# The even layer's TensorE order, written out: attention in clusters between whole channel products

## The chip, the cores and the metric

The kernel runs on one core of a Trainium2 chip. The metric is the time of one execution in microseconds, the median of several; lower is better. The engines are named as in the profile: PE (TensorE matmuls), PEld (its weight loads), DVE (VectorE), ACT (ScalarE), POOL (GpSimd) and SP (SyncE, which here only issues DMAs).

## The reference

One inference step of two layers for 384 tokens: 256 of a prompt and 8 samples of 16. The change lies in the mixer of the first (even) layer:

```python
def even_mixer(h, ck, cv, clogf, sconv_state, w_in, conv_w, q_gain, k_gain, b_f, w_out):
    proj = h @ w_in
    gate_b, gate_c, u, q, k, v, f_logit = jnp.split(proj, cuts, axis=-1)
    conv_out, new_sconv = causal_dwconv(gate_c * u, sconv_state, conv_w)
    a_out = gate_b * conv_out
    q = rms_norm(q.reshape(hs), q_gain)
    k = rms_norm(k.reshape(hs), k_gain)
    ...
    attn = fox_attention(q, k_all, v_all, logf_all, n_past).reshape(b, length, FOX_WIDTH)
    out = jnp.concatenate([a_out, attn.astype(a_out.dtype)], axis=-1) @ w_out
```

So one half is a gated short convolution over 512 channels, the other an attention of 8 heads of 64 with a decay: the score of query and key gets the difference of their summed log-forget values, is masked causally, and goes through a softmax. The prompt attends to itself (256 x 256 a head), each sample to its 128 cached keys and its own 16. After the mixer come a feed-forward block (FFN), then the odd layer and its FFN; these are the same in both kernels.

## The kernel before

All activations lie feature-major: 128 channels on the partitions, 384 tokens along the free axis. A product in full precision is made of three matmuls: activations and weights are split into a high part that PE takes in its fast format (Hh, wh) and a rest (Hl, wl), and `three` adds wh·Hh, wh·Hl and wl·Hh. A weight tile of 128 x 1024 comes by a DMA on SP (raw), ACT rounds it (wh), DVE subtracts (wl). raw, wh and wl have three buffers each, and one tile holds the weights of one whole channel product.

The even layer, in the order of its source:

- q, k and v, token-major, by `tm_group`: eight weight pieces of 512 columns for three token tiles each. `qk` squares and sums the heads, scales, and leaves q and k in SBUF (the tiles qraw, kraw). `to_features` transposes them on PE (qT, kT), four 128x128 a token tile; ACT writes QT and KTt. POOL then scales kraw in place and stores it (o_k); ACT writes vt from v, POOL stores it (o_v).
- `short_conv(i)`, i from 0 to 3: three channel products of 24 matmuls each (gc, gu, gb), 128 x 384, and then the convolution on DVE, ACT and POOL (tiles cu, cpad, cc, cg, ca), which writes rows 0 to 3 of yh and yl, the two parts of the output projection's input.
- Prompt attention by blocks. The first has 128 queries, 128 keys, and all 8 heads; the second block of queries has 256 keys, and two groups of four heads. A block's scores (s) lie in two PSUM banks, one for the even heads and one for the odd (`par`): the decay (cumP with nid8R, or cum0 with onesR), the mask (causR with identR), and then KTt with QT, 64 rows of the array for each parity. DVE takes the maximum (mx), ACT the exponential with its sum (pr), DVE the reciprocal (rs) and the scaling (pr); PE transposes pr (pt), DVE copies it out (pts), and PE multiplies by vt (po), 64 columns of the array for each parity.
- The samples: scores in groups of three, three and two (ss), softmax (prs), transposes (pt, pn), the products with cached and new values (pa), and transposes of the result (aoT), which end in rows 4 to 7 of yh and yl.
- The output projection op, eight tiles of 24 matmuls, in halves: rows 0 to 3 and rows 4 to 7.

Each attention step has several calls of `fill`, which would draw channel products from the generator `beside_attention`. Its ratio FILL_E is 0.0, so all of them are written behind attention, by `fill.rest()`. A scheduler that works on the written program decides the order on each engine: PE's order before is its choice. `T.keep` ties PE's instructions to the source order where it is set; it is not set in the kernel before. Weight tiles are made at high priority.

The pools: `e1` holds what is needed up to v (kraw, krow, lfA among them), `e2` takes its memory afterwards and holds what convolution and attention need (onesR, cum0, cpad, pr and others), so e2's first tiles wait for the last use of e1's, o_k's DMAs among them. Eight PSUM banks: four for large products (`pmm`: v, gc, gu, gb, op) and four for the rest (`paux`: kT, s, pt, po, ss, pa).

Of the kernel before, what the change touches and what calls it, by code (L numbers as in the profile page):

```python
# [10 lines left out]
F32 = mybir.dt.float32  # L11
# [219 lines left out]
def build(nc, tc, d, stop=None):  # L231
# [38 lines left out]
    def paux(name):  # L270
        return psum["aux"].tile([P, 512], F32, tag="aux", name=name)
# [11 lines left out]
    def prc(name, i):  # L283
        o = COL[name] + i
        return prm[:, o:o + 1]
# [10 lines left out]
    def f32(ap):  # L296
        return ap.bitcast(F32)

    def tt(out, a, b, op, eng=None):
        (eng or V).tensor_tensor(out=out, in0=a, in1=b, op=op)  # L300
# [4 lines left out]
    def act(out, a, f, **kw):  # L305
        S.activation(out, a, f, **kw)  # L306
# [294 lines left out]
    def to_features(src, name, fill=None):  # L601

        ps = paux(name)
        for i in range(4):
            T.transpose(ps[:, i * P:(i + 1) * P], src[:, i * P:(i + 1) * P], ident)
        if fill:
            fill(4)
        return ps.rearrange("p (k t) -> p k t", t=P)
# [39 lines left out]
                    rows = slice(64 * half, 64 * half + 64)  # L648
                    V.tensor_scalar_mul(Qb[rows, kt, :, 16 * half:16 * half + 16], tok_s(ps[rows, kt, :]), qg8[rows, :])
    k = qk("k")  # L650
    for b in range(3):
        ps = to_features(k[:, b, :], "kT")
        act(KTt[:, :, b * P:(b + 1) * P], ps, AF.Copy, scale=prc("kg", 0))
        tt(k[:, b, :], k[:, b, :], krow, ALU.mult, G)
        nc.gpsimd.dma_start(out=d["o_k"][b], in_=k[:, b, :])

    ps = run(tm_group("v"))
    for b in range(3):
        act(vt[:, b, :], ps[b], AF.Copy, scale=r[:, b:b + 1])
        nc.gpsimd.dma_start(out=d["o_v"][b], in_=vt[:, b, :])  # L660
    e1s.close()

    e2s = ExitStack()
    e2 = e2s.enter_context(tc.tile_pool(name="e2", bufs=2))

    def short_conv(i):
        pg, pu, pb = pmm("gc"), pmm("gu"), pmm("gb")
# [36 lines left out]

    fill = Fill(beside_attention(), FILL_E)

    def softmax(ps3, out3, sums):

        n = len(sums)
        nm = tiny.tile([P, n], F32, tag="mx", name="mx")  # L710
        V.reduce_max(out=nm, in_=ps3, axis=AX.X, negate=True)
        for i in range(n):
            act(out3[:, i, :], ps3[:, i, :], AF.Exp, bias=nm[:, i:i + 1], accum_out=sums[i])
# [6 lines left out]
        tt(cum0[:, par, :, :], f32(cumP[:, 0:P]).unsqueeze(1).broadcast_to([P, 4, P]),  # L720
           C("nid8")[:, par::2].unsqueeze(2).broadcast_to([P, 4, P]), ALU.mult)

    for qb in range(2):
        nk = P * (qb + 1)
        nh = 512 // nk
        po = paux("po").rearrange("p (k t) -> p k t", t=P)
        for h0 in range(0, 8, 2 * nh):
            banks = [paux("s").rearrange("p (h k) -> p h k", k=nk) for _ in range(2)]
            for par in range(2):
                if qb == 0:  # L730
                    T.matmul(banks[par], lhsT=onesR, rhs=cum0[:, par, :, :], start=True, stop=False)
                    fill()
                else:
                    for i in range(nh):
                        h = h0 + 2 * i + par
                        T.matmul(banks[par][:, i, :], lhsT=nid8R[:, h:h + 1].broadcast_to([P, P]), rhs=cumP[:, 0:nk],
                                 start=i == 0, stop=False)
                        fill()
                T.matmul(banks[par][:, :, nk - P:nk], lhsT=identR, rhs=causR.unsqueeze(1).broadcast_to([P, nh, P]),
                         start=False, stop=False)  # L740
                fill()
            for i in range(nh):
                for par in range(2):
                    kt = (h0 + 2 * i) // 2
                    rows = slice(64 * par, 64 * par + 64)
                    T.matmul(banks[par][:, i, :], lhsT=QT[rows, kt, qb * P:(qb + 1) * P], rhs=KTt[rows, kt, 0:nk],
                             start=False, stop=i == nh - 1)
                    fill()
            pts = []
            for par in range(2):  # L750
                pr = e2.tile([P, nh, nk], F32, tag="pr", name="pr")
                sm = tiny.tile([P, nh], F32, tag="sm", name="sm")
                softmax(banks[par], pr, [sm[:, i:i + 1] for i in range(nh)])
                rs = tiny.tile([P, nh], F32, tag="rs", name="rs")
                V.reciprocal(rs, sm)
                tt(pr, pr, rs.unsqueeze(2).broadcast_to([P, nh, nk]), ALU.mult)
                pt = paux("pt")
                for i in range(nh):
                    for kb in range(qb + 1):
                        o = (i * (qb + 1) + kb) * P  # L760
                        T.transpose(pt[:, o:o + P], pr[:, i, kb * P:(kb + 1) * P], ident)
                        fill()
                ptt = e2.tile([P, 512], F32, tag="pts", name="pts", bufs=3)
                V.tensor_copy(ptt, pt)
                pts.append(ptt)
            for i in range(nh):
                kt = h0 // 2 + i
                for kb in range(qb + 1):
                    o = (i * (qb + 1) + kb) * P
                    for par in range(2):  # L770
                        h = 2 * kt + par
                        T.matmul(po[64 * par:64 * par + 64, kt, :], lhsT=vt[:, kb, 64 * h:64 * h + 64],
                                 rhs=pts[par][:, o:o + P], start=kt == 0 and kb == 0, stop=kt == 3 and kb == qb)
                        fill()
        o = slice(qb * P, (qb + 1) * P)
        act(yh[:, 4:8, o], po, AF.Copy)
        tt(yl[:, 4:8, o], po, f32(yh[:, 4:8, o]), ALU.subtract)


    pn = e2.tile([P, NB, LB], F32, name="pn", bufs=1)  # L780
    pTp = e2.tile([P, NB, P], F32, name="pTp", bufs=1)
    rS = e2.tile([P, NB], F32, name="rS", bufs=1)
    for b0 in range(0, NB, 3):
        nb = min(3, NB - b0)
        ps = paux("ss")
        s3 = ps[:, :nb * 144].rearrange("p (b k) -> p b k", k=144)
        T.matmul(ps[:, :nb * 144], lhsT=nidSR, rhs=cumS[:, 144 * b0:144 * (b0 + nb)], start=True, stop=False)
        fill()
        T.matmul(s3[:, :, P:144], lhsT=identR, rhs=smaskR.unsqueeze(1).broadcast_to([P, nb, LB]), start=False, stop=False)
        fill()  # L790
        for i in range(nb):
            b = b0 + i
            kc = e0.tile([P, 4, P], F32, tag="kvc", name="kc", bufs=4)
            nc.sync.dma_start(out=kc, in_=d["kc"][b])
            for new in range(2):
                for kt in range(4):
                    rows = slice(32 * kt, 32 * kt + 32)
                    if new:
                        T.matmul(s3[rows, i, P:144], lhsT=Qb[:, kt, b, :], rhs=KTt[:, kt, 256 + LB * b:256 + LB * (b + 1)],
                                 start=False, stop=i == nb - 1)  # L800
                        fill()
                    else:
                        T.matmul(s3[rows, i, 0:P], lhsT=Qb[:, kt, b, :], rhs=kc[:, kt, :], start=False, stop=False)
                        fill()
        pr = e2.tile([P, nb, 144], F32, tag="prs", name="prs")
        sm = tiny.tile([P, nb], F32, tag="sms", name="sms")
        softmax(s3, pr, [sm[:, i:i + 1] for i in range(nb)])
        V.reciprocal(rS[:, b0:b0 + nb], sm)
        V.tensor_copy(pn[:, b0:b0 + nb, :], pr[:, :, P:144])
        pt = paux("pt")  # L810
        for i in range(nb):
            T.transpose(pt[:, i * P:(i + 1) * P], pr[:, i, 0:P], ident)
            fill()
        V.tensor_copy(pTp[:, b0:b0 + nb, :], pt[:, :nb * P].rearrange("p (b k) -> p b k", k=P))
    ps = paux("pn")
    T.transpose(ps[:, 0:P], pn.rearrange("p b t -> p (b t)"), ident)
    fill()
# [2 lines left out]
    pTm = e2.tile([P, NB, P], F32, name="pTm", bufs=1)  # L820
    for b in range(NB):
        V.tensor_scalar_mul(pTm[:, b, :], pnT, C("bmask")[:, b:b + 1])
    for j in range(2):
        pa = paux("pa")
        for i in range(4):
            b = 4 * j + i
# [2 lines left out]
            for new in range(2):  # L829
                for kt in range(4):  # L830
# [2 lines left out]
                    T.matmul(pa[32 * kt:32 * kt + 32, i * P:(i + 1) * P], lhsT=lhs, rhs=rhs,  # L833
                             start=i == 0 and not new, stop=i == 3 and new == 1)
                    fill()
        ao = e2.tile([P, 4, P], F32, tag="ao", name="ao", bufs=1)
        tt(ao, pa.rearrange("p (b c) -> p b c", c=P), rS[:, 4 * j:4 * j + 4].unsqueeze(2).broadcast_to([P, 4, P]), ALU.mult)
        ps = paux("aoT")
        for i in range(4):
            T.transpose(ps[:, i * P:(i + 1) * P], ao[:, i, :], ident)  # L840
            fill()
        for half in range(2):
# [4 lines left out]
            act(oh, src, AF.Copy)  # L847
            tt(yl[rows, 4:8, o].rearrange("p k (b t) -> p k b t", t=LB), src, f32(oh), ALU.subtract)

    fill.rest()  # L850
    for m0 in (0, 4):
        ps = ops if m0 == 0 else [pmm("op") for _ in range(4)]
        for m in range(4):
            if m0:
                run(fm_group(ps[m], yh, yl, range(0, 4), True, False))
        for m in range(4):
            run(fm_group(ps[m], yh, yl, range(4, 8), False, True))
            residual(m0 + m, ps[m])
            norm_tile(m0 + m, "g_ffn", 0, e2)
# [496 lines left out]
```

## Time and profile before

| | |
|---|---|
| median of 3 runs | 1062.48 us (1061.84 to 1063.17) |
| the profiled execution | 1065.19 us, of which 1063.4 is the span of its instructions |
| granted PE clock, mean | 0.995 |
| PE, PEld, DVE, ACT, POOL busy | 98%, 91%, 70%, 48%, 10% of the span |
| even layer from v's end to the FFN's first matmul | 65.24 to 183.62 us |

A row of the timeline gives the start in us from the span's start, the length in us, the engine, the line, the operation, out<-in by tile names without buffer numbers, the shapes, and the count; in brackets the idle time of that engine before it and what ended it. Matmuls are pipelined, so the lengths of neighbours overlap: what one costs PE is the distance from its start to the next start. A matmul in f32 shows as two records. All matmuls are made by `Tensor.matmul`, on line 240 (transposes on 245), so a matmul is told by its tiles. L300 is the two-tensor operation of DVE or POOL, L303 its form with a scalar, L306 any ACT operation. A row of the table by stretches has the stretch, its length, busy time (and count) of PE, PEld, DVE, ACT and POOL, PE's granted clock, the share of the DMA engines and GB/s.

### The profile page before, as it was taken

What the parts mean: (1) busy time and instruction counts of PE and PEld (TensorE: products, weight loads), DVE (VectorE), ACT (ScalarE), POOL (GpSimd) and SP (SyncE); (2) the same over time, 40 slices, a digit from 0 to 9 for tenths busy, and PEclk for the clock granted to TensorE, in tenths of its full rate; (3) what the DMA queues carried; (4) which work ended last, traced back from release to release, by engine and by line L of the source; (5) the groups of instructions that cost most, each with busy time, mean ns of one, the idle gap of its engine ahead of it and who ended that gap; (6) DMA issues with size and microseconds to landing.
All of it is one profiled execution on the core that took longest, in us unless ns stands there. A gap on an engine that the chain in (4) does not pass through costs nothing.

```text
span 1063.4 us, 16718 instructions
## 1 busy us (share of the span) xinstructions
PE 1039.9 (98%) x6316; PEld 969.7 (91%) x6316; DVE 739.8 (70%) x1361; ACT 511.6 (48%) x855; POOL 104.4 (10%) x339
## 2 busy tenths in 40 slices
PE   9999999999999999999899999899999999999998
PEld 6788799999999999989678888787989999999998
DVE  6967657777777734458989979868987776665331
ACT  5444335444444433346968668364544444443221
POOL 0030010100000000013313112210001100000000
PEclk9999999999999999999999999999999999999999
DMA  7542434344343443435555463553533434434541
GB/s 261 170 158 81 160 112 128 126 122 137 119 132 127 130 136 119 126 108 167 188 187 190 159 198 130 190 179 103 179 125 120 127 120 123 133 122 135 151 136 43
DMA packets 50329, 150.31 MB, mean 141 GB/s; under 512 B 5992, under 2 KB 8312, under 8 KB 50248
## 3 DMA queue, kind: packets, MB, share of 16 engines
q1 hardware_dynamic: 44360, 136.78, 40.9%
q10 hardware_dynamic: 4608, 8.39, 2.1%
q0 software_dynamic: 1280, 4.06, 1.0%
q8 instruction: 50, 0.82, 0.3%
q14 instruction: 31, 0.25, 0.1%
HBM read 135.81 MB, written 13.40 MB: 140 GB/s over the span
## 4 chain that ended last, share of the span: by engine, by line
PE 38%; DVE 13%; ACT 3%; issue 2%; DMA 0%; ACTq 0%; DVEq 0%
PE fg L240 9%; PE fd L240 9%; PE fa L240 8%; PE z L240 4%; PE xbc L240 3%; DVE wl L300 2%; DVE c L303 2%; PE op L240 2%; DVE wl L303 1%; DVE X L300 1%; ACT wh L306 1%; PE y L240 1%; DVE pad L300 1%; PE S L240 0%; ACT L306 0%
## 5 line engine op out<-in xcount | busy, mean ns | idle before, releaser
L300 DVE TENSOR_TENSOR wl<-raw,wh 128x1024 fp32r<-128x1024 f32 (+1 forms) x205 | 252.5, 1232 | 140.6 <-ACT wh L306 140.1
L306 ACT ACTIVATE wh<-raw 128x1024 fp32r<-128x1024 f32 (+1 forms) x205 | 216.0, 1054 | 225.0 <-PE fd L240 95.0
L240 PE MATMUL fg<-Hh,wh 128*128 128x384 f32 x352 | 119.0, 338 | 1.0 <-DVE pad L300 1.0
L240 PE MATMUL fa<-Hl,wh 128*128 128x384 f32 x352 | 119.3, 339 | 0.6 <-DVE Hl L303 0.6
L240 PE MATMUL fg<-Hl,wh 128*128 128x384 f32 x352 | 119.2, 339 | 0.0
L240 PE MATMUL fa<-Hh,wl 128*128 128x384 f32 x352 | 119.0, 338 | 0.0
L240 PE MATMUL fg<-Hh,wl 128*128 128x384 f32 x352 | 119.0, 338 | 0.0
L240 PE MATMUL fa<-Hh,wh 128*128 128x384 f32 x352 | 118.9, 338 | 0.0
L240 PE MATMUL fd<-hh,wh 128*128 128x384 f32 x352 | 118.3, 336 | 0.0
L240 PE MATMUL fd<-hh,wl 128*128 128x384 f32 x352 | 118.3, 336 | 0.0
L240 PE MATMUL fd<-hl,wh 128*128 128x384 f32 x352 | 118.3, 336 | 0.0
L303 DVE SCALAR_TENSOR_TENSOR c<-pad,prm,c 128x400 f32<-128x400 f32 (+1 forms) x160 | 101.9, 645 | 7.9 <-ACT c L306 6.2
L240 PEld LDWEIGHTS fg<-Hh,wh 128*128 128x128 f32 x352 | 66.2, 188 | 1.3 <-ACT R L306 1.3
L240 PEld LDWEIGHTS fa<-Hl,wh 128*128 128x128 f32 x352 | 66.1, 188 | 1.1 <-DVE Hl L303 0.9
L240 PE MATMUL xbc<-Hh,wh 128*128 128x384 f32 x192 | 65.9, 343 | 0.7 <-DVE X L300 0.7
L240 PEld LDWEIGHTS fa<-Hh,wl 128*128 128x128 f32 x352 | 66.2, 188 | 0.1
L240 PEld LDWEIGHTS fg<-Hl,wh 128*128 128x128 f32 x352 | 66.2, 188 | 0.1
L240 PEld LDWEIGHTS fg<-Hh,wl 128*128 128x128 f32 x352 | 66.2, 188 | 0.1
L240 PEld LDWEIGHTS fa<-Hh,wh 128*128 128x128 f32 x352 | 66.1, 188 | 0.1
L240 PEld LDWEIGHTS fd<-hh,wh 128*128 128x128 f32 x352 | 66.2, 188 | 0.0
L240 PEld LDWEIGHTS fd<-hl,wh 128*128 128x128 f32 x352 | 66.2, 188 | 0.0
L240 PEld LDWEIGHTS fd<-hh,wl 128*128 128x128 f32 x352 | 66.2, 188 | 0.0
(737 smaller groups left out, 2108.1 us busy)
## 6 DMA issues: line engine op xcount, KB each, us to landing
raw<-w SPq DMA_DIRECT2D x219, 512.0 KB, 3.5
kc<-kc SPq DMA_DIRECT2D x8, 256.0 KB, 3.5
vc<-vc SPq DMA_DIRECT2D x8, 256.0 KB, 3.0
X<-x SPq DMA_DIRECT2D x8, 192.0 KB, 4.7
o_y<-X SPq DMA_DIRECT2D x8, 192.0 KB, 2.8
o_v<-vt POOLq DMA_DIRECT2D x3, 256.0 KB, 2.5
o_k<-kraw POOLq DMA_DIRECT2D x3, 256.0 KB, 3.3
cst<-cst SPq DMA_DIRECT2D x1, 617.0 KB, 5.9
```

Source lines behind the costliest of these rows:

```text
L240: ins = nc.tensor.matmul(*a, **kw)
L300: (eng or V).tensor_tensor(out=out, in0=a, in1=b, op=op)
L303: V.scalar_tensor_tensor(out=out, in0=a, scalar=s, in1=b, op0=op0, op1=op1)
L306: S.activation(out, a, f, **kw)
```

## The change

From v on, PE's instructions are tied to the source order, and the source is written in the order wanted. `dense()` draws eight pieces from `beside_attention`, that is one whole channel product; the attention steps stand between, as `Heads(qb, h0)` (scores and softmax of one block), `turn` (transposes) and `out` (values), and as `scores`, `turn_scores`, `samples_out` and `turn_out` for the samples. v is written ahead of k's transposes, and kraw's pool closes behind them. pr gets four buffers instead of two, ao two instead of one.

```diff
     k = qk("k")
-    for b in range(3):
-        ps = to_features(k[:, b, :], "kT")
-        ...
     ps = run(tm_group("v"))
     for b in range(3):
         act(vt[:, b, :], ps[b], AF.Copy, scale=r[:, b:b + 1])
         nc.gpsimd.dma_start(out=d["o_v"][b], in_=vt[:, b, :])
-    e1s.close()
...
+    def dense(n=8):
+        for _ in range(n):
+            next(fill.gen, None)
+
+    T.keep = True
+    dense()
+    for b in range(3):
+        ps = to_features(k[:, b, :], "kT")
+        act(KTt[:, :, b * P:(b + 1) * P], ps, AF.Copy, scale=prc("kg", 0))
+        tt(k[:, b, :], k[:, b, :], krow, ALU.mult, G)
+        nc.gpsimd.dma_start(out=d["o_k"][b], in_=k[:, b, :])
+
+    e1s.close()
+
+    e2s = ExitStack()
+    e2 = e2s.enter_context(tc.tile_pool(name="e2", bufs=2))
+    dense(16)
...
+    class Heads:
+        def __init__(self, qb, h0):
...
+            for i in range(nh):
+                for par in range(2):
+                    T.matmul(banks[par][:, i, :], lhsT=QT[rows, kt, ...], rhs=KTt[rows, kt, 0:nk], ...)
...
+    first = Heads(0, 0)
+    dense()
+    second = Heads(1, 0)
+    first.turn()
+    dense()
+    po = pout()
+    first.out(po)
+    second.turn()
+    dense()
+    third = Heads(1, 4)
+    po = pout()
+    second.out(po)
+    dense()
+    third.turn()
...
+    s0 = scores(0)
+    dense()
+    third.out(po)
+    s1 = scores(3)
+    turn_scores(*s0)
+    dense()
+    s2 = scores(6)
+    turn_scores(*s1)
+    dense()
+    turn_scores(*s2)
...
+    dense()
+    a0 = samples_out(0)
+    dense()
+    a1 = samples_out(1)
+    turn_out(*a0)
+    dense()
+    turn_out(*a1)
     fill.rest()
+    T.keep = False
```

Three places show how the instructions move. The first is PE behind v's last matmul. Before, where v_640 is v's third token tile:

```order
L240 MATMUL v_640<-wl,Hh 128x512
L240 MATMUL v_640<-wh,Hl 128x512
L240 MATMUL gc<-Hh,wh 128x384
L245 MATMUL kT<-cst,kraw 128x128 x4
L240 MATMUL gc<-Hl,wh 128x384
L245 MATMUL kT<-cst,kraw 128x128 x4
L240 MATMUL gc<-Hh,wl 128x384
L245 MATMUL kT<-cst,kraw 128x128 x4
```

In the change, the end of the first gc product and the start of gu:

```order
L240 MATMUL gc<-Hh,wh 128x384
L240 MATMUL gc<-Hl,wh 128x384
L240 MATMUL gc<-Hh,wl 128x384
L245 MATMUL kT<-cst,kraw 128x128 x12
L240 MATMUL gu<-Hh,wh 128x384
```

The twelve transposes stand behind the whole gc product instead of behind its first matmul.

The second is DVE ahead of the first block's decay, between the scaling of kraw and cum0 (cum_749 before, cum_842 in the change). Before:

```order
L300 TENSOR_TENSOR kraw<-kraw,hs_609 128x512 x3
L300 TENSOR_TENSOR wl<-raw,wh 128x1024 x3
L717 CAST onesR<-cst 128x128
L300 TENSOR_TENSOR cum_749<-cumP,cst 128x512
L300 TENSOR_TENSOR wl<-raw,wh 128x1024
L300 TENSOR_TENSOR cum_749<-cumP,cst 128x512
```

In the change:

```order
L300 TENSOR_TENSOR kraw<-kraw,hs_609 128x512 x3
L300 TENSOR_TENSOR wl<-raw,wh 128x1024 x4
L726 CAST onesR<-cst 128x128
L300 TENSOR_TENSOR cum_842<-cumP,cst 128x512 x2
L300 TENSOR_TENSOR cu<-gu,R_232 128x384
```

One more weight tail stands ahead of onesR and cum0.

The third is PE at the second block. Before, from the second bank of the first block's transposes on:

```order
L245 MATMUL pt<-cst,pr 128x128 x4
L240 MATMUL gu<-Hh,wh 128x384
L240 MATMUL po<-pts,vt 64x128
L240 MATMUL s<-cumP,nid8R 128x256 x2
L240 MATMUL s<-causR,identR 128x2x128
L240 MATMUL s<-cumP,nid8R 128x256 x2
L240 MATMUL s<-causR,identR 128x2x128
L240 MATMUL s<-KTt,QT 128x256 x2
L240 MATMUL po<-pts,vt 64x128 x7
L240 MATMUL s<-KTt,QT 128x256 x2
L240 MATMUL gu<-Hl,wh 128x384
```

In the change, from the end of the second gc product on:

```order
L240 MATMUL gc<-Hh,wl 128x384
L240 MATMUL s<-cumP,nid8R 128x256 x2
L240 MATMUL s<-causR,identR 128x2x128
L240 MATMUL s<-cumP,nid8R 128x256 x2
L240 MATMUL s<-causR,identR 128x2x128
L240 MATMUL s<-KTt,QT 128x256 x4
L245 MATMUL pt<-cst,pr 128x128 x8
L240 MATMUL gu<-Hh,wh 128x384
```

The block's scores stand in one piece, with the first block's eight transposes behind them; its po follows after the whole gu product. The eight KTt matmuls of the first block, four of one parity and then four of the other before, alternate between the parities in the change.

More of the change, by code (lines that the diff above doesn't have):

```diff
@@ L650, in build @@
     k = qk("k")
-    for b in range(3):
-        ps = to_features(k[:, b, :], "kT")
-        act(KTt[:, :, b * P:(b + 1) * P], ps, AF.Copy, scale=prc("kg", 0))
-        tt(k[:, b, :], k[:, b, :], krow, ALU.mult, G)
-        nc.gpsimd.dma_start(out=d["o_k"][b], in_=k[:, b, :])
     ps = run(tm_group("v"))
@@ L660, in build @@
         nc.gpsimd.dma_start(out=d["o_v"][b], in_=vt[:, b, :])
-    e1s.close()
-    e2s = ExitStack()
-    e2 = e2s.enter_context(tc.tile_pool(name="e2", bufs=2))
     def short_conv(i):
@@ L721, in build @@
            C("nid8")[:, par::2].unsqueeze(2).broadcast_to([P, 4, P]), ALU.mult)
[L723 to L728, printed above, removed]
+    class Heads:
+        def __init__(self, qb, h0):
+            self.qb, self.h0, self.nk = qb, h0, P * (qb + 1)
+            self.nh = nh = 512 // self.nk
+            nk = self.nk
+            self.banks = banks = [paux("s").rearrange("p (h k) -> p h k", k=nk) for _ in range(2)]
             for par in range(2):
@@ L731, in build @@
                     T.matmul(banks[par], lhsT=onesR, rhs=cum0[:, par, :, :], start=True, stop=False)
-                    fill()
                 else:
@@ L747, in build @@
                              start=False, stop=i == nh - 1)
-                    fill()
-            pts = []
+            self.prs = []
             for par in range(2):
-                pr = e2.tile([P, nh, nk], F32, tag="pr", name="pr")
+                pr = e2.tile([P, nh, nk], F32, tag="pr", name="pr", bufs=4)
                 sm = tiny.tile([P, nh], F32, tag="sm", name="sm")
@@ L756, in build, with turn, out @@
                 tt(pr, pr, rs.unsqueeze(2).broadcast_to([P, nh, nk]), ALU.mult)
+                self.prs.append(pr)
+        def turn(self):
+            self.pts = []
+            for pr in self.prs:
                 pt = paux("pt")
-                for i in range(nh):
-                    for kb in range(qb + 1):
-                        o = (i * (qb + 1) + kb) * P
+                for i in range(self.nh):
+                    for kb in range(self.qb + 1):
+                        o = (i * (self.qb + 1) + kb) * P
                         T.transpose(pt[:, o:o + P], pr[:, i, kb * P:(kb + 1) * P], ident)
-                        fill()
                 ptt = e2.tile([P, 512], F32, tag="pts", name="pts", bufs=3)
                 V.tensor_copy(ptt, pt)
-                pts.append(ptt)
-            for i in range(nh):
-                kt = h0 // 2 + i
+                self.pts.append(ptt)
+        def out(self, po):
+            qb = self.qb
+            for i in range(self.nh):
+                kt = self.h0 // 2 + i
                 for kb in range(qb + 1):
@@ L772, in build, with pout @@
                         T.matmul(po[64 * par:64 * par + 64, kt, :], lhsT=vt[:, kb, 64 * h:64 * h + 64],
[L773 to L777, printed above, removed]
+                                 rhs=self.pts[par][:, o:o + P], start=kt == 0 and kb == 0, stop=kt == 3 and kb == qb)
+            if self.h0 // 2 + self.nh == 4:
+                o = slice(qb * P, (qb + 1) * P)
+                act(yh[:, 4:8, o], po, AF.Copy)
+                tt(yl[:, 4:8, o], po, f32(yh[:, 4:8, o]), ALU.subtract)
+    def pout():
+        return paux("po").rearrange("p (k t) -> p k t", t=P)
+    first = Heads(0, 0)
[12 more added lines that the diff above has]
+    third.turn()
     pn = e2.tile([P, NB, LB], F32, name="pn", bufs=1)
@@ L782, in build, with scores @@
     rS = e2.tile([P, NB], F32, name="rS", bufs=1)
-    for b0 in range(0, NB, 3):
+    def scores(b0):
         nb = min(3, NB - b0)
@@ L809, in build, with turn_scores @@
         V.tensor_copy(pn[:, b0:b0 + nb, :], pr[:, :, P:144])
+        return b0, nb, pr
+    def turn_scores(b0, nb, pr):
         pt = paux("pt")
@@ L822, in build, with samples_out @@
         V.tensor_scalar_mul(pTm[:, b, :], pnT, C("bmask")[:, b:b + 1])
-    for j in range(2):
+    def samples_out(j):
         pa = paux("pa")
@@ L835, in build, with turn_out @@
                     fill()
-        ao = e2.tile([P, 4, P], F32, tag="ao", name="ao", bufs=1)
+        ao = e2.tile([P, 4, P], F32, tag="ao", name="ao", bufs=2)
         tt(ao, pa.rearrange("p (b c) -> p b c", c=P), rS[:, 4 * j:4 * j + 4].unsqueeze(2).broadcast_to([P, 4, P]), ALU.mult)
+        return j, ao
+    def turn_out(j, ao):
         ps = paux("aoT")
```

2 lines of the change are left out of this document (removed).

## The prediction

> **What bounds the kernel now.** I read the page first, then a table of the even layer by stretches, then the timeline of TensorE (PE) there, then the other engines where PE waits.
>
> ```profile
> span 1063.4 us, 16718 instructions
> PE 1039.9 (98%) x6316; PEld 969.7 (91%) x6316; DVE 739.8 (70%) x1361; ACT 511.6 (48%) x855; POOL 104.4 (10%) x339
> ...
> 65.24:84.42 19.18, 16.98 (x94) 16.58 (x93) 9.04 (x16) 7.07 (x9) 8.41 (x13) 0.91 0.59 192
> 84.42:133.40 48.98, 48.80 (x512) 39.36 (x512) 35.05 (x75) 18.60 (x61) 1.77 (x8) 1.00 0.35 119
> 133.40:183.62 50.22, 50.22 (x289) 49.85 (x289) 32.36 (x50) 21.52 (x31) 3.17 (x5) 1.00 0.39 119
> ```
>
> PE is busy for 98% of the span, so time is won only by shortening what PE does or waits for. The change moves work from the end of v (65.24) to the feed-forward's first matmul (183.62): 118.4 us. The columns after the length are PE, PEld, DVE, ACT and POOL busy, PE's granted clock, the DMA share and GB/s. The first stretch alone has idle time and a lower clock.
>
> "Busy" hides cost here, because a record covers a matmul's whole passage; what it costs is the distance to the next start.
>
> ```profile
> 74.71 0.34 PE L240 MATMUL gu<-Hh,wh 128*128 128x384 f32 x1
> ...
> 83.03 0.34 PE L240 MATMUL gc<-Hh,wh 128*128 128x384 f32 x1
> ```
>
> Two whole products (gu, gb: 48 matmuls) take 8.32 us: 0.173 us a matmul, 4.16 us a product. Of 288 channel matmuls 80 precede 84.42 and 96 follow 133.40; the other 112 take 19.4 of the middle stretch's 49.0 us. The remaining 29.6 us are attention and the switches to and from it.
>
> **The place that waits now.** Part kT:
>
> ```profile
> 65.24 0.34 PE L240 MATMUL gc<-Hh,wh 128*128 128x384 f32 x1
> 67.78 0.63 PE L245 MATMUL kT<-cst,kraw 128*128 128x128 f32 x4 [2.20 <-DVE kraw L300]
> 70.39 0.52 PE L240 MATMUL gc<-Hl,wh 128*128 128x384 f32 x1
> 70.71 0.52 PE L240 MATMUL gc<-Hh,wl 128*128 128x384 f32 x1
> ...
> 65.41:68.82 3.41, 1.21 (x11) 1.05 (x10) 3.19 (x11) 1.46 (x3) 1.05 (x3) 1.00 0.79 234
> 68.82:72.23 3.41, 3.41 (x14) 3.34 (x13) 2.23 (x2) 2.26 (x4) 3.41 (x3) 0.50 0.28 83
> ...
> 66.94 1.90 DVE L300 TENSOR_TENSOR kraw<-kraw,hs 128x512 f32<-128x512 f32 x3
> ```
>
> After one gc matmul PE sits 2.20 us for the scaled k. Then the clock is 0.50 for 3.41 us (matmuls 0.32 us apart), which costs up to 1.7 us. With a whole gc product (4.16 us) ahead of kT, PE arrives at 69.4; DVE has the last k tile at 68.84. This wait goes: -2.2 us. The cover is thin, 0.5 us.
>
> **What the clusters save on PE.** Rows of the timeline:
>
> ```profile
> 84.97 1.16 PE L240 MATMUL s<-KTt,QT 64*128 64x128 f32 x8
> 86.06 0.44 PE L240 MATMUL gc<-Hh,wl 128*128 128x384 f32 x1
> 86.34 0.34 PE L240 MATMUL gc<-Hh,wh 128*128 128x384 f32 x1
> ...
> 93.63 0.70 PE L240 MATMUL s<-KTt,QT 64*128 64x256 f32 x4
> 94.26 1.09 PE L240 MATMUL po<-pts,vt 128*64 128x128 f32 x14
> ...
> 102.45 1.13 PE L240 MATMUL s<-KTt,QT 64*128 64x256 f32 x6
> 103.51 1.09 PE L240 MATMUL po<-pts,vt 128*64 128x128 f32 x14
> 104.52 0.70 PE L240 MATMUL s<-KTt,QT 64*128 64x256 f32 x2
> 105.15 0.44 PE L240 MATMUL gb<-Hh,wl 128*128 128x384 f32 x1
> ...
> 108.69 0.46 PE L240 MATMUL ss<-cumS,nidSR 64*128 64x432 f32 x1
> 109.08 0.43 PE L240 MATMUL po<-pts,vt 128*64 128x128 f32 x2
> 109.44 0.29 PE L240 MATMUL ss<-smaskR,identR 128*128 128x48 f32 x1
> 109.66 0.43 PE L240 MATMUL ss<-kc,Qb 128*32 128x128 f32 x8
> 109.91 0.23 PE L240 MATMUL ss<-KTt,Qb 128*32 128x16 f32 x8
> 109.97 0.41 PE L240 MATMUL ss<-kc,Qb 128*32 128x128 f32 x8
> ...
> 118.46 0.27 PE L245 MATMUL pt<-cst,prs 128*128 128x128 f32 x1
> ...
> 120.86 0.44 PE L240 MATMUL gc<-Hh,wl 128*128 128x384 f32 x1
> ```
>
> - Scores (s). The trace counts two records per f32 matmul. A lone 256-wide one costs 0.63 us (104.52 to 105.15); three, whose parities alternate 0, 1, 0, cost 1.06 (102.45). So a second on the other 64 rows is free, and a next turn costs 0.43. Four 128-wide of one parity take 1.09 (84.97 to 86.06), and two such runs stand there now. The change lists parities in turn: eight 128-wide are four turns, 1.09 instead of 2.18. The four of each later block are two turns, 1.06 each, where now one block takes 2 x 0.63 (93.63 to 94.26) and the other 1.06 + 0.63. Together 5.13 - 3.21 = -1.9 us (0 if 128-wide ones do not pair).
> - po. Seven matmuls take 1.01 us; the eighth stands alone, 0.36 us (109.08 to 109.44), three times. In one run it falls into the fourth turn: -1.1 us (0 if not).
> - Sample scores (ss) and their transposes. A sample's eight matmuls cost 0.31 (109.66 to 109.97), a block's head 0.39 + 0.22. Now block three, two samples with the transposes of block two mixed in, takes 2.4 us (118.46 to 120.86). Unbroken it is 0.6 + 0.6, and 0.4 for three transposes, estimated: 0.8 less. Block two is broken in the same way; it, block one and the last transposes I put at 0.6 together: -1.4 us (0.7 to 1.8).
> - pa stands in two runs instead of eight: six switches fewer, which I put at -0.4 us.
> - Returns. The first large matmul after an attention run takes 0.28 instead of 0.17 (86.06 to 86.34). I count 23 returns now and 12 in the change: -1.1 us.
>
> Sum: -5.9 us, between 2.5 and 7.
>
> **What the fixed order adds.** Nothing may slip into a wait any more, so I walked each cluster for what it needs, with durations from rows. One waits.
>
> Before the first score matmul DVE must make onesR and cum0. In the change four weight tails (wl) stand ahead of them on DVE, not three. The fourth goes into the buffer that gb's own weights hold (three buffers; gc, gu, gb), so its ACT half cannot start before gb's last matmuls. The same chain one product earlier shows its length:
>
> ```profile
> 78.87 0.34 PE L240 MATMUL gb<-Hh,wh 128*128 128x384 f32 x1
> ...
> 78.90 1.06 ACT L306 ACTIVATE wh<-raw 128x1024 fp32r<-128x1024 f32 x1 [3.10 <-PE gu L240]
> ...
> 79.99 1.22 DVE L300 TENSOR_TENSOR wl<-raw,wh 128x1024 fp32r<-128x1024 f32 x1 [2.93 <-ACT wh L306]
> 81.27 0.68 DVE L300 TENSOR_TENSOR cum<-cumP,cst 128x512 fp32r<-128x512 f32 x1
> ```
>
> From gu's end (78.87) to cum0 (81.27 + 0.68 = 81.95) are 3.1 us. Now gb covers them. In the change they start at gb's end, near 79, and nothing covers them: s, and every matmul behind it, waits until about 82.1: +3.1 us. Had that wl stood behind, o_k's landing would hold onesR (it uses k's memory): DVE's cost would be near 0.7, my lower end. The upper is 4.8, with the clock below.
>
> The clock: a stretch with 1.21 us busy of 3.41 is followed by 0.50 above. After 3.1 us idle I expect the same again, a loss of up to 1.7 us at the new place for the one that goes at the old. I count both as equal, 0.
>
> The other clusters have slack. The tightest is the third block's transposes:
>
> ```profile
> 96.63 1.28 DVE L711 TENSOR_REDUCE mx<-s 128x2 f32<-128x512 f32 x2
> ...
> 99.57 0.69 DVE L300 TENSOR_TENSOR pr<-pr,rs 128x512 f32<-128x512 f32 x1
> ```
>
> From the two maxima's start to the last pr are 3.6 us now (96.63 to 100.26). In the change a wl (1.1 ACT, then 1.2 DVE) stands ahead of them: the last pr is ready 5.9 us after gb's end. PE takes 0.1 + 1.95 (s) + 1.1 (po) + 0.1 + 4.16 (gc) = 7.4: 1.5 us to spare; the first two blocks have more. In the sample half, each transpose has a product between; pa waits for eight pTm behind a wl, with half a us to spare by my count; the first output product reaches the fourth channel's rows some 4 us after gb, and their yl, behind one wl and the second ao, is there 0.3 us earlier. On SP the cache loads wait for their buffers 4 us or more before use, and the weight loads queued behind them are needed later still. On POOL three o_v stores move ahead of k's scaling, at no one's wait. v keeps its place on PE. All at 0, hidden by the 4.16 us products.
>
> Sum: -5.9 - 2.2 + 3.1 = -5.0 us. The profiled execution took 1065.19 (1063.4 span and 1.8 around it), 2.7 above the median of the three runs, 1062.48; from it 1060.2, from the median **1057.5 us**. A difference under 0.2% (2.1 us) can't be told from none.
>
> **Rivals.**
> 1. The clock stays. The windows whose boundaries the clock's records show:
>
> ```profile
> 676.40:679.81 3.41, 1.56 (x9) 1.25 (x8) 3.41 (x6) 0.56 (x1) 1.55 (x3) 1.00 0.74 231
> 679.81:683.22 3.41, 1.47 (x8) 1.47 (x9) 2.81 (x6) 1.17 (x4) 0.00 (x0) 1.00 0.69 233
> 683.22:686.63 3.41, 3.41 (x14) 1.57 (x12) 0.56 (x1) 1.06 (x1) 0.00 (x0) 0.50 0.02 5
> ```
>
> Busy 1.56 kept it, 1.47 lost it. An idle of 3.1 us keeps it only if a boundary cuts it near its middle (0.7 of 3.41 positions, 2 in 10). Then the old loss goes and no new one comes: 1057.5 - 1.7 = 1055.8. Chance 0.2.
> The Trainium skill, "TensorE: Matmul & The Clock Gate", Part 1, says the clock halves after a whole idle window of about 3.4 us, by which 3.1 us would keep it and this rival would be the likely one. The trace differs: 2.20 us idle sufficed at 65.6.
>
> 2. The small matmuls gain less in a row: 128-wide ones do not pair (1.9 and 1.1 lost). For it: 64x128 never alternates now. Against: po's seven in 1.01 us do. 1057.5 + 3.0 = 1060.5, next to no change. Chance 0.17.
>
> 3. Slower: softmax comes late for the transposes. If the exponentials and conv steps queue so that the three blocks' pr come 9 us after the product instead of 6, each of three clusters waits 1.5 and may lose its clock, 1.7: 1057.5 + 9.6 = 1067.1. It begins when the chain exceeds 7.4 us, and turns the sign where the three clusters lose 5 us together. Against: durations of rows, and DVE busy 35 of 49 us there. Chance 0.06.
>
> 4. The first wait is short (0.7): 1055.1, or less with the clock kept. Chance 0.06.
>
> **How the numbers follow.** My case within 1.5 us has 0.5. The range reaches from rivals 1 and 4 less their spread (1053.5) to rival 2 plus 0.5 (1061.0). Faster: 0.5 + 0.2 + 0.06 and half of rival 2, 0.83; same 0.11; slower 0.06.
>
> **What would show it.** After: no wait ahead of kT, one of about 3 us ahead of the first s, ended by DVE cum, with a half-speed stretch behind it; eight KTt matmuls in about 1.1 us; feed-forward from about 178.5. Waits ahead of pt or pa, or half clock in other clusters, would prove me wrong.

## The result and the profile after

The changed kernel takes 1056.87 us (median of four, 1056.59 to 1057.57) beside 1062.21 for the kernel before (four, 1061.84 to 1063.17): a ratio of 0.9949, 95% interval 0.9932 to 0.9967, so faster by 5.3 us. Predicted were 1057.5 and a range of 1053.5 to 1061.0. Two more sets of runs, beside the experiments, gave ratios of 0.9953 (0.9939 to 0.9966) and 0.9947 (0.9933 to 0.9961). The medians leave out two executions that ran in a slow state, one of the changed kernel (4667 us, the profiled one of the first set below, so no trace of it is read) and one of the run with pieces inside (1140 us).

The head of the page of the changed kernel, and the even layer by stretches (columns as before; the first stretch ends where the first score matmul starts, the last at the feed-forward's first matmul):

```profile
span 1055.8 us, 16715 instructions
PE 1031.8 (98%) x6316; PEld 965.3 (91%) x6316; DVE 740.0 (70%) x1361; ACT 510.7 (48%) x855; POOL 103.8 (10%) x339
...
64.15:81.14 16.99, 13.98 (x85) 13.64 (x84) 9.73 (x17) 6.74 (x9) 8.31 (x13) 1.00 0.67 217
81.14:132.00 50.86, 50.85 (x443) 46.37 (x444) 37.76 (x75) 21.66 (x63) 3.62 (x10) 0.97 0.36 115
132.00:176.56 44.56, 44.56 (x366) 43.62 (x366) 28.61 (x50) 18.17 (x28) 1.85 (x3) 1.00 0.43 137
```

From v's end to the feed-forward were 118.4 us; now they are 176.56 - 64.15 = 112.4, 6.0 less. PE is as full as before (98%): it does the same 6316 matmuls in less time. The span is 7.6 us shorter; 1.1 of that lies ahead of the section (v ends at 64.15 where it ended at 65.24) and 0.5 behind it, at places that the change doesn't touch. So the section's length is what the steps are held against. It is read from one execution of each kernel, and a second one of the changed kernel gave 113.2 for 112.4, so a difference under 1 us between two sections says little.

TensorE's timeline, at the place that waited before and at the one that waits now:

```profile
68.33 1.47 PE L245 MATMUL kT<-cst,kraw 128*128 128x128 f32 x12
69.55 0.42 PE L240 MATMUL gu<-Hh,wh 128*128 128x384 f32 x1
...
81.14 0.47 PE L240 MATMUL s<-cum,onesR 128*128 128x512 f32 x1 [3.01 <-DVE cum L300]
...
82.92 2.08 PE L240 MATMUL s<-KTt,QT 64*128 64x128 f32 x16
84.93 0.44 PE L240 MATMUL gc<-Hh,wh 128*128 128x384 f32 x1
...
PE s L240 <- DVE cum L300: 3.0, 1, 3.0
```

The last line is the whole list of PE's waits in the section. kT no longer waits: twelve transposes in one run, 1.2 us to the next product. The first score matmul waits 3.01 us, ended by DVE's cum, and nothing else waits. What stands ahead of cum, on ACT and DVE:

```profile
77.99 1.06 ACT L306 ACTIVATE wh<-raw 128x1024 fp32r<-128x1024 f32 x1 [3.10 <-PE gb L240]
...
79.08 1.23 DVE L300 TENSOR_TENSOR wl<-raw,wh 128x1024 fp32r<-128x1024 f32 x1 [2.93 <-ACT wh L306]
80.22 0.22 DVE L726 CAST onesR<-cst 128x128 fp32r<-128x128 f32 x1
80.36 1.29 DVE L300 TENSOR_TENSOR cum<-cumP,cst 128x512 fp32r<-128x512 f32 x2
```

It is the chain of the prediction: the fourth weight piece's ACT half starts at gb's end, its DVE half follows, and only then do the constants come, which need nothing of it.

The clock's windows there (the last three numbers are granted clock, DMA share and GB/s):

```profile
78.13:81.55 3.42, 0.41 (x3) 0.30 (x2) 2.47 (x4) 0.92 (x1) 0.42 (x4) 1.00 0.49 132
81.55:84.96 3.41, 3.41 (x21) 2.32 (x19) 1.65 (x5) 0.63 (x1) 0.39 (x2) 0.50 0.34 133
```

A window with 0.41 us of work is followed by one at half clock, in which the first block's eight KTt products take 2.01 us. The later blocks, at full clock:

```profile
89.99 1.14 PE L240 MATMUL s<-KTt,QT 64*128 64x256 f32 x8
91.05 1.09 PE L245 MATMUL pt<-cst,pr 128*128 128x128 f32 x8
...
96.31 1.09 PE L240 MATMUL po<-pts,vt 128*64 128x128 f32 x16
97.34 1.09 PE L245 MATMUL pt<-cst,pr 128*128 128x128 f32 x8
```

Four 256-wide KTt products take 1.06 us, eight po products 1.03.

### The profile page after: what moved, and what is told of

It reads as the page before. It is cut to its first block, busy times and chain, and to the rows that moved or that the text cites. A ratio compares the mean times of both kernels' runs of the same rounds, so it can differ in the third digit from the quotient of the medians.

```text
span 1055.8 us, 16715 instructions
## 1 busy us (share of the span) xinstructions
PE 1031.8 (98%) x6316; PEld 965.3 (91%) x6316; DVE 740.0 (70%) x1361; ACT 510.7 (48%) x855; POOL 103.8 (10%) x339
## 4 chain that ended last, share of the span: by engine, by line
PE 38%; DVE 13%; ACT 3%; issue 2%; DMA 1%; ACTq 0%; DVEq 0%
PE fd L240 9%; PE fg L240 9%; PE fa L240 8%; PE z L240 4%; PE xbc L240 3%; PE op L240 2%; DVE wl L300 2%; DVE c L303 2%; DVE wl L303 1%; DVE X L300 1%; PE y L240 1%; ACT wh L306 1%; DVE pad L300 1%; PE S L240 0%; PE yi L240 0%
## 5 line engine op out<-in xcount | busy, mean ns | idle before, releaser
L240 PE MATMUL fg<-Hh,wh 128*128 128x384 f32 x352 | 118.4, 336 | 1.0 <-DVE pad L300 1.0
L240 PE MATMUL fa<-Hh,wl 128*128 128x384 f32 x352 | 118.4, 336 | 0.0
L240 PE MATMUL fg<-Hh,wl 128*128 128x384 f32 x352 | 118.4, 336 | 0.0
```

The source lines that it names most:

```text
L240: ins = nc.tensor.matmul(*a, **kw)
```

## The experiments

All runs, by the median; "section" is from v's end to the feed-forward's first matmul in the profiled execution. They ran in three sets, each with the kernel before beside it: the first has the changed kernel, kT's step alone, kT first and the constants early on DVE; the second has scores by halves, po by halves, pieces inside and the constants on POOL, but not the changed kernel; the third has the changed kernel and k's buffer apart.

| kernel | us (lowest to highest, runs) | ratio to before, 95% | section, us |
|---|---|---|---|
| before | 1061.5 (26, beside the second set) | 1 | 118.4 |
| after, first set | 1057.06 (1054.78 to 1058.14, 5) | 0.9953, 0.9939 to 0.9966 | |
| after, third set | 1056.03 (1055.30 to 1058.52, 6) | 0.9947, 0.9933 to 0.9961 | 113.2 |
| kT's step alone | 1058.56 (1056.30 to 1059.34, 6) | 0.9969, 0.9957 to 0.9981 | 114.0 |
| after, kT first | 1056.88 (1055.14 to 1058.22, 6) | 0.9954, 0.9942 to 0.9966 | 113.8 |
| scores by halves | 1058.85 (1056.63 to 1060.75, 12) | 0.9977, 0.9965 to 0.9988 | 115.9 |
| po by halves | 1057.68 (1054.68 to 1059.45, 10) | 0.9964, 0.9950 to 0.9978 | 112.7 |
| pieces inside | 1066.26 (1064.07 to 1073.30, 12) | 1.0034, 1.0017 to 1.0051 | 124.6 |
| constants early, DVE | 1054.05 (1052.66 to 1055.81, 6) | 0.9928, 0.9914 to 0.9941 | 112.4 |
| constants on POOL | 1055.59 (1054.54 to 1056.13, 6) | 0.9943, 0.9926 to 0.9960 | 112.3 |
| k's buffer apart | 1050.69 (1049.99 to 1052.05, 5) | 0.9893, 0.9878 to 0.9908 | 108.2 |

The changed kernel stood in two sets as the measure:

> The changed kernel once more, beside the others of this set: about 1056.9 us. It is what they are measured against; from the first channel product to feed-forward's first matmul about 112.4 us, with a wait of 3.0 us ahead of the first s.

> The changed kernel beside the next one: 1056.5 to 1057.3 us, with the wait of 3.0 us ahead of the first s.

Both came as expected to within half a microsecond (1057.06 and 1056.03).

**kT's step alone.** The kernel before, with kT moved behind v and one whole product, and PE tied to the source order only as far as kT; e1 closes behind it (shown without the lines that go from the old place):

```diff
+    T.keep = True
+    for _ in range(8):
+        next(fill.gen, None)
     for b in range(3):
         ps = to_features(k[:, b, :], "kT")
...
+    T.keep = False
```

> Before, with one step of the change alone: kT's transposes behind one whole channel product in source order; the attention itself keeps before's loops and the scheduler's order. My theory: the wait ahead of kT (2.2 us in before) goes and nothing takes its place, since 17 channel matmuls, about 4 us, now lie ahead of the first s and cover the fourth wl: 2.2 us less than before, up to 3.9 if its stretch of half clock goes too, so 1058.3 to 1060.0 us. Rival: this step is worth nothing, because the wait only moves from kT to the first s: 1061.5 to 1062.5 us. By my theory the rest of the change (3 to 5 us) is the pairing and clustering of attention's matmuls, less the new wait.

Measured 1058.56: 2.9 us less than before, within the range. Its profile lists no wait of PE in the section at all, and the clock stays:

```profile
63.68:177.66 113.98, 113.85 (x893) 103.77 (x892) 75.62 (x140) 46.71 (x100) 12.75 (x26) 1.00 0.44 136
```

DVE has the four weight tails ahead of the constants here too, but the free scheduler puts 17 matmuls of the next gc product ahead of the first s, and they cover the chain. So the step is worth its 2.2 us of waiting and the stretch of half clock (up to 1.7), 4.4 us of the section by these two executions; the new wait is not its price, but that of tying the scores to the source order right behind gb.

**kT first.** After, with kT's transposes ahead of the first product:

```diff
     T.keep = True
-    dense()
     for b in range(3):
         ps = to_features(k[:, b, :], "kT")
...
-    dense(16)
+    dense(24)
```

> After, with kT's transposes moved back ahead of the first channel product, and all three products behind them. My theory: the wait ahead of kT comes back, 2.2 to 2.6 us, with half clock behind it; on VectorE only three wl stand ahead of the constants then, so the wait ahead of the first s falls to between 0 and 1 us and its half clock goes: between 0.8 us less and 1.0 us more than after, 1056.1 to 1057.9 us, the one wait in place of the other. Rival: the two waits are independent, so the first comes on top of the second: 1059 us or more.

Measured 1056.88: 0.2 less than after beside it, in the range. PE's waits in the section, and the windows round the first of them:

```profile
PE kT L245 <- DVE kraw L300: 2.4, 1, 2.4
PE po L240 <- DVE pts L773: 1.0, 2, 0.8
PE pa L240 <- DMA vc<-vc: 0.4, 1, 0.4
...
63.61:67.02 3.41, 1.02 (x7) 0.57 (x6) 3.19 (x9) 2.36 (x4) 1.08 (x2) 1.00 0.54 160
67.02:70.44 3.42, 3.42 (x16) 3.26 (x15) 2.97 (x3) 2.06 (x3) 2.81 (x4) 0.50 0.51 200
```

The wait ahead of kT is back and the one ahead of s is gone: one stands for the other. The section is 4.6 us shorter than before with the same kind of wait in both, so this is the rest of the change, the clusters, with 1.4 us of small waits of its own. Without those waits, which after doesn't have, the clusters are worth 6.0. The pieces then add up to about what the section of after shows: -4.4 (kT, with its clock) - 6.0 (clusters) + 3.0 (wait ahead of s) + up to 1.7 (its clock) = -5.7 to -7.4 us, for -6.0.

**Scores by halves.** After, KTt's products of each cluster listed one half of the array after the other:

```diff
-            for i in range(nh):
-                for par in range(2):
+            for par in range(2):
+                for i in range(nh):
```

> After, with the KTt matmuls of each score cluster listed one half of the array after the other (all of par 0, then all of par 1) in place of alternating. My theory: alternating halves run beside each other, in after 8 of 256 columns in 1.06 us; listed by half they run one by one, 0.86 us more for each of the two later clusters and 1.1 us for the first: about 2.8 us more than after, 1059.5 to 1060.2 us. Rival: the cluster gains because nothing interrupts it, not because its halves alternate: no change, 1056.9 us.

Measured 1058.85: 1.8 to 2.8 us more than the three medians of after, below the range. The timeline tells why:

```profile
82.42 3.09 PE L240 MATMUL s<-KTt,QT 64*128 64x128 f32 x16
85.44 0.69 PE L240 MATMUL gc<-Hh,wh 128*128 128x384 f32 x1
...
92.61 1.14 PE L240 MATMUL s<-KTt,QT 64*128 64x256 f32 x8
93.68 0.33 PE L245 MATMUL pt<-cst,pr 128*128 128x128 f32 x1
```

The first cluster costs 3.02 us for 2.01, both at half clock. The later ones cost 1.07 for 1.06: nothing. So halves do run beside each other, but two products of each half need no alternation for it, and four of each lose only half of what I had put down: 1.0 us at half clock, which would be about 0.5 at full clock (an estimate). The trace also has two more windows at half clock here (three in a row from 79.8), so the time of this run doesn't tell the price; the rows do. The twelve runs had mean clocks of 0.988 to 0.993, where those of after had 0.991 to 0.995, so most of them seem to have such windows; why is not shown.

**po by halves.** The same edit for po:

```diff
-            for i in range(self.nh):
-                kt = self.h0 // 2 + i
-                for kb in range(qb + 1):
-                    o = (i * (qb + 1) + kb) * P
-                    for par in range(2):
+            for par in range(2):
+                for i in range(self.nh):
+                    kt = self.h0 // 2 + i
+                    for kb in range(qb + 1):
+                        o = (i * (qb + 1) + kb) * P
```

> After, with the po matmuls of each cluster listed one half of the array after the other. In after 16 of 128 columns stand in 1.03 us. My theory: pairs of column halves run beside each other and lose that here, some 0.87 us in each of three clusters: 2.6 us more than after, 1059.3 to 1060.0 us. Rival: po's two halves write different rows of one bank and gain from being uninterrupted alone: no change, 1056.9 us.

Measured 1057.68: 0.6 to 1.7 us more than the three medians of after, less than my theory's 2.6. The intervals of the two ratios overlap, so here too the rows decide, not the time. A cluster's rows, and its matmuls counted by stretches (PE busy and, in brackets, the records that fall in it, also in part; two records a product) here and, last, in after:

```profile
94.46 1.58 PE L240 MATMUL po<-pts,vt 128*64 128x128 f32 x16
95.97 1.09 PE L245 MATMUL pt<-cst,pr 128*128 128x128 f32 x8
...
94.45:94.94 0.49, 0.48 (x4) 0.48 (x5) 0.00 (x0) 0.00 (x0) 1.00 0.00 0
94.94:95.40 0.46, 0.46 (x10) 0.46 (x9) 0.00 (x0) 0.00 (x0) 1.00 0.00 0
95.40:95.97 0.57, 0.57 (x8) 0.40 (x4) 0.00 (x0) 0.00 (x0) 1.00 0.10 29
...
96.31:96.80 0.49, 0.49 (x8) 0.49 (x10) 0.00 (x0) 0.00 (x0) 1.00 0.00 0
```

1.51 us for 1.03, in all three clusters alike: 1.45 in sum, not 2.6. In the first half microsecond four records run alone, where after has eight in pairs; then both halves run beside each other (ten records); then the second half's rest is alone again. The second half's products begin once no more than four records of the first are still to start. Twelve steps take the place of eight, where sixteen would be one by one: 1.51 / 1.03 = 1.47. The 128-wide scores show the same 12 for 8 (3.02 / 2.01 = 1.50), and with four records of each half nothing is lost. Three cases fit; that it is a depth of four records is my reading of them.

**Pieces inside.** After, with one piece of a channel product for every eight matmuls of the sample clusters:

```diff
-FILL_E = 0.0
+FILL_E = 0.125
```

> After, with the channel products' pieces back inside the sample clusters (ss, pa): one piece of three matmuls of 384 columns for every eight of attention's, in place of none. The prompt clusters stay whole. My theory: each of the about 18 further switches costs some 0.11 us for the return and about as much for the entry, and pieces split groups of four that ran beside each other: 2 to 5 us more than after, 1059 to 1062 us. Rival: what counts is pairing in the prompt clusters alone, and returns cost nothing that lasts: within 1 us of after.

Measured 1066.26, 9 to 10 us more than after and slower than before: the direction holds, the size fails. The profiled execution is the slowest of the twelve (1073.30), so what follows tells where time goes, not how much of the median. First a row of its timeline on each side of a piece, then its waits behind the first s:

```profile
112.73 0.45 PE L240 MATMUL gu<-Hh,wh 128*128 128x384 f32 x1
113.02 0.34 PE L240 MATMUL gu<-Hl,wh 128*128 128x384 f32 x1
113.20 0.34 PE L240 MATMUL gu<-Hh,wl 128*128 128x384 f32 x1
113.47 0.21 PE L240 MATMUL ss<-KTt,Qb 128*32 128x16 f32 x2
...
PE op L240 <- ACT yh L306: 2.0, 2, 1.4
PE aoT L245 <- DVE ao L300: 1.3, 1, 1.3
```

A piece between attention's matmuls takes 0.29 + 0.18 + 0.27 us (112.73 to 113.47) where three channel matmuls in a row take 0.52: 0.22 for going out and back. I count 27 returns, 15 more than in after (not 18), so 3.3 us. The rest I had not expected: the drawn pieces bring the output projection forward to where its inputs aren't ready (2.0 us ahead of op, 1.3 ahead of aoT). With the windows of half clock, two more than in after, these sum to some 10 of the section's 12.2 us. Of the rest, about 1.0 lies in the sample scores themselves, as the split groups of the theory would have it: from start to start ss takes 5.39 us for 4.39 in after.

**Constants early, on DVE.** After, with onesR and cum0 built right behind cumP, ahead of q, and in e0:

```diff
+    onesR = e0.tile([P, P], F32R, name="onesR", bufs=1)
+    V.tensor_copy(onesR, C("ones")[:, 0:P])
+    cum0 = e0.tile([P, 2, 4, P], F32R, name="cum0", bufs=1)
+    ...
-    onesR = e2.tile([P, P], F32R, name="onesR", bufs=1)
-    ...
```

> The constants of the first scores (onesR, cum0) are built right behind cumP, ahead of q's transposes; TensorE's order is that of after. My theory: the wait of 3.0 us ahead of the first s is the price of standing behind the fourth wl on VectorE, so it goes whole, and with it the stretch of half clock behind it (2.01 us for matmuls that are worth 1.0 at full clock, so up to 1.7 us over the window of 3.41): 1052.2 to 1053.9 us. Rival: the scores would next wait for KTt or for another operand, and little comes of it: 1056 us or more.

Measured 1054.05, 3.0 us less than after beside it, a hair above the range. The wait ahead of s is gone, but another came:

```profile
PE kT L245 <- DVE kraw L300: 1.7, 2, 1.0
...
68.10 2.36 DVE L300 TENSOR_TENSOR kraw<-kraw,hs 128x512 f32<-128x512 f32 x2
...
71.38:74.79 3.41, 3.41 (x13) 3.41 (x12) 1.30 (x1) 0.58 (x1) 3.10 (x5) 0.50 0.59 161
```

The 1.3 us of constants now stand ahead of k on DVE, a weight tail (66.97, 1.22 us) has slipped in behind k's first tile, k's last two tiles are ready at 70.46 where PE arrives at 67.6, and the clock halves behind it. In the profiled execution the section is no shorter than in after (112.4 both); the gain seen there lies behind it (877.0 us to the span's end for 879.2), where one window of half clock follows each of two old idle stretches instead of two. So of the 3 us at most about 1.3, the difference of the two waits, can be this edit's, and the section doesn't show even that; the rest is not shown to be.

**Constants on POOL.** After, with onesR and cum0 on POOL, in e0:

```diff
+    G.tensor_copy(onesR, C("ones")[:, 0:P])
...
+        tt(cum0[:, par, :, :], f32(cumP[:, 0:P]).unsqueeze(1).broadcast_to([P, 4, P]),
+           C("nid8")[:, par::2].unsqueeze(2).broadcast_to([P, 4, P]), ALU.mult, G)
```

> After, with onesR and cum0 built on GpSimd while v's product runs, so that neither the four wl nor k's factor shares VectorE's row with them; TensorE's order is that of after. When they stood early on VectorE, the wait ahead of the first s went, but one of 1.7 us ahead of kT came with a stretch of half clock. My theory: here neither is there: 3.0 us of waiting and up to 1.7 us of clock less than after, 1051.5 to 1053.9 us, and less than with the constants early on VectorE. Rival: GpSimd slows VectorE while both work, k's factor comes late all the same, and the wait ahead of kT is 1 to 2 us again: 1054 us or more.

Measured 1055.59: neither the theory's range nor the rival's reason. Neither kT nor s waits; s starts at 77.48. The time is lost one cluster on:

```profile
87.88 0.63 PE L245 MATMUL pt<-cst,pr 128*128 128x128 f32 x4 [2.09 <-issue]
89.21 0.68 PE L245 MATMUL pt<-cst,pr 128*128 128x128 f32 x4 [0.71 <-DVE pr L300]
...
78.51 0.56 DVE L300 TENSOR_TENSOR cu<-gu,R 128x384 f32<-128x384 f32 x1 [6.89 <-DMA o_k<-kraw]
```

The first transposes wait 2.8 us, since the softmax is late, and a window of half clock follows (from 89.65). DVE had stood idle for 6.89 us ahead of cu, which writes into e2's memory and so waits for k's store out of e1, until 78.51; the weight tails, the convolution and the maxima queued behind it. So the constants were only the first of e2's tiles to be held up. That showed what to change.

**k's buffer apart.** After, with k in the pool that stays open (q keeps the one buffer in e1):

```diff
-        raw = e1.tile([P, 3, 512], F32, tag="qk", name=name + "raw", bufs=2)
+        raw = (e0 if name == "k" else e1).tile([P, 3, 512], F32, tag="qk", name=name + "raw", bufs=1)
```

> After, with k's buffer in the pool that stays open (e0) in place of the one that closes ahead of attention (e1). No instruction is added or taken away, and TensorE's and ScalarE's order stay as in after; on VectorE onesR and cum0 now stand behind three wl in place of four, and before cu. My theory: the constants could not be built early because their pool takes the memory of e1, which k's last transfer out still reads (it lands at 78.3 us in after); with k apart they are ready at about 77.6 us, when TensorE has just finished gb. The wait ahead of the first s falls from 3.0 us to 0 to 0.5, none comes at kT, and none of 2.8 us at the first pt as when GpSimd built the constants, since cu no longer stands behind that transfer either: 3 us less than after, up to 1.7 more with the clock, 1052 to 1054 us, and at least as fast as every other kernel of this study. Rival: the softmax, not the constants, is the next to be late, and the time goes to the first pt as it did there: 1055 to 1056 us.

Measured 1050.69, 5.3 us less than after beside it and below the range; 0.9893 of before. DVE and PE:

```profile
74.09 1.23 DVE L300 TENSOR_TENSOR wl<-raw,wh 128x1024 fp32r<-128x1024 f32 x1 [3.55 <-ACT wh L306]
75.24 0.25 DVE L726 CAST onesR<-cst 128x128 fp32r<-128x128 f32 x1
75.38 1.32 DVE L300 TENSOR_TENSOR cum<-cumP,cst 128x512 fp32r<-128x512 f32 x2
76.73 0.56 DVE L300 TENSOR_TENSOR cu<-gu,R 128x384 f32<-128x384 f32 x1
...
77.13 0.40 PE L240 MATMUL s<-cum,onesR 128*128 128x512 f32 x1
...
63.32:171.50 108.18, 107.77 (x893) 102.68 (x892) 76.14 (x140) 46.55 (x100) 13.93 (x26) 1.00 0.45 144
```

The constants are ready at 76.7, ahead of gb's end; no wait at kT, s or pt, and full clock: the section is 4.2 us shorter. Of these 3.0 are the wait; the window of half clock (up to 1.7), less a wait of 0.4 ahead of pa that the profile of after doesn't have, fits the other 1.2. Its profiled execution gains 1.8 us more behind the section (877.4 us for 879.2), again one window of half clock for two at both of the later idle stretches (4.63 and 3.77 us long, as in after). Whether the edit shifts those windows or they fell so by chance stays open (the last section shows what their number goes by): the five runs had mean clocks of 0.993 to 0.997, the eleven of after beside the experiments 0.991 to 0.995.

## Why the prediction was right, step by step

- **The wait ahead of kT (-2.2).** Right: it is gone, and undoing or keeping this step alone moves it as foreseen. The clock that goes with it makes the step worth more by itself (4.4 us of the section).
- **The new wait ahead of s (+3.1).** Right: 3.01 us, ended by cum, behind the fourth wl. The last run shows its root to be one step further back: moving k's buffer alone put the constants ahead of the fourth wl. That the scheduler had put them behind because their memory was not yet free is the reading that fits; the run doesn't show the scheduler's reasons.
- **The clock (0).** Right for the section: one window of half clock goes at kT, one comes at s. Behind the section, for which the prediction put nothing, the profile of after has two such windows more than that of before. By the rule of the Trainium skill that the prediction weighed ("TensorE: Matmul & The Clock Gate", Part 1: a whole idle window is needed), the wait of 3.01 us should have left the clock alone; this trace disagrees. But the positions do matter, as in the first rival: with po by halves the same wait of 3.0 us fell across a boundary, and no halving followed. Of the five profiled executions with this wait it is the only one without, near the 2 in 10 of the prediction:

```profile
76.05:79.46 3.41, 1.64 (x10) 1.32 (x8) 0.82 (x1) 1.06 (x1) 0.41 (x4) 1.00 0.73 221
79.46:82.88 3.42, 2.17 (x20) 1.50 (x20) 3.30 (x8) 0.01 (x1) 0.22 (x2) 1.00 0.47 156
```

- **Clusters on PE (-5.9).** Right in sum, a little small. Between the starts of the matmuls, before against the last run (where the clock is full): KTt 5.12 to 3.22 us (-1.9, as put), po 4.14 to 3.07 (-1.1, as put), ss 5.48 to 4.39 with the samples' transposes 1.60 to 0.85 (-1.8 for -1.4), pa 4.18 to 3.77 in after (-0.4). Of the section's 10.2 us between these two, 2.0 are waits and 1.7 the window of half clock; 6.5 remain for all clusters and returns. The returns are 23 before and 12 in after, as counted.
- **Where its reasoning failed.** The prediction gave the scores' gain to the list that alternates the halves. For the two 256-wide blocks the runs show that it comes from standing in one piece; only the 128-wide block, and po, need the list, and lose half of the pairing without it. That a second matmul on the other rows is free holds. The sign of eight KTt matmuls in about 1.1 us shows in the last run (1.1); in after they took 2.01, at the half clock that the prediction itself had put there.
- **The other clusters' slack (0).** Right in the first profile, where the wait ahead of s is the only one of PE in the section, but not safe: in the second profiled execution of the same kernel PE waits 0.5 us ahead of pa for the load of vc, a wait that the prediction named as a sign of being wrong (it had the cache loads released 4 us or more before their use). The third rival's mechanism is real, too: with the constants on POOL it took 2.8 us.
- **The sum (-5.0).** The section gave 6.0 in the profile and the medians 5.3; the difference from the forecast, 0.6 us by the median, is below what can be told. As windows of half clock move single executions by more than that, so near a hit is partly luck. In the chances, 0.5 + 0.2 + 0.06 and half of 0.17 are 0.845, where 0.83 is written.

## What to carry to other kernels

When instructions of one engine are tied to an order, the waits that a scheduler had filled come back: walk every operand of the first instruction at each place, and on its producer's engine everything that stands ahead of it, needed or not. If such a producer can't be moved, look for what holds its memory: one buffer moved to another pool gave more here than moving the work itself to another time or engine. And a step's price is better read from the start-to-start distances of a run of its own than from the run's time, since windows of half clock elsewhere move the time by 1 to 3 us.

## What the runs showed of the hardware that I had not expected

- Matmuls on two halves of the array, listed one half after the other, overlap all the same once four records (two products) or fewer of the first half are outstanding: 12 steps for 8, and no loss at all with four records a half. The Trainium skill, in "TensorE: Matmul & The Clock Gate", Part 3, says that weight loads are pulled ahead but matmuls start in strict program order; in the run with po by halves, where PE is tied to the order of the list, ten records fall in the middle 0.46 us, as only both halves side by side give (eight in 0.49 us in after), so here a matmul of the second half started before the last ones of the first.
- Busy time alone doesn't say whether the clock stays. Windows of 1.47 us busy (before) and 0.41 (after) lost it, 1.56 and 1.64 kept it; but with the constants early on DVE a window that was 1.68 busy, most of it transposes of k, was followed by half clock:

```profile
67.96:71.38 3.42, 1.68 (x13) 1.26 (x12) 3.42 (x4) 2.12 (x4) 3.06 (x2) 1.00 0.57 204
```

- The same idle stretches of the later stage, 4.6 and 3.8 us, were followed by one window of half clock in some executions and by two in others, which is worth up to 1.7 us each and can't be told from an edit's own effect in a few runs. Their number goes by where the windows' boundaries cut the stretch. The first window at half clock behind the 4.6 us, in after (two windows) and with k's buffer apart (one):

```profile
515.04:518.45 3.41, 2.67 (x33) 2.29 (x34) 3.41 (x6) 3.41 (x8) 0.00 (x0) 0.50 0.43 167
...
510.60:514.01 3.41, 3.27 (x34) 2.29 (x34) 3.41 (x7) 3.41 (x8) 0.00 (x0) 0.50 0.41 123
```

In all eleven profiled executions that are read here, and at both stretches, it is so: where PE was busy for 3.27 us or more of the first window at half clock, that window was the only one; where it was busy for 0.88 to 2.67 us, because the idle stretch reached into it, a second one followed. In the section one window breaks this rule, in the run with scores by halves: from 83.21 PE is busy throughout at half clock, partly with the unpaired matmuls, and the next window is at half clock all the same.
